# State-space heads: score products run two heads at a time, decays on ScalarE, and GpSimd low parts with later transposes in the expert search

## The chip, the cores and the metric

One core of one Trainium2 chip runs the whole kernel. The metric is device time in microseconds (us) of one execution; lower is better. TensorE has two clock levels here, 1.2 and 2.4 GHz; the profile writes the granted clock as a share of 2.4 GHz.

## What is computed

256 tokens (and 16 meta tokens ahead of them) of width 1024 pass through a hybrid layer (a gated linear attention and a state-space mixer, "SSD"), a layer of product-key experts ("PEER"), and a second block of retention and stick-breaking attention. Two parts of it matter here. The SSD's core, for a chunk:

```python
acum = jnp.cumsum(a, axis=1)
seg = jnp.exp(-jnp.abs(acum[:, :, None] - acum[:, None, :]))
cb = jnp.einsum('btgn,bsgn->btsg', Cc, Bc)
y = jnp.einsum('btsgr,btsg,bsgrp->btgrp', seg, cb, xdt)
y = y + jnp.einsum('btgn,bgrpn,btgr->btgrp', Cc, S, jnp.exp(acum))
```

There are 32 heads in 4 groups of 8. And the search of the experts: for each token and head the 16 best of 128 first keys and of 128 second keys, and of their sums the 16 best again:

```python
s = jnp.einsum('nhid,hikd->nhik', q, sub_keys).astype(jnp.float32)
s_top, i_top = lax.top_k(s, PEER_TOPK)
cand = s_top[:, :, 0, :, None] + s_top[:, :, 1, None, :]
best, pos = lax.top_k(cand.reshape(n, PEER_HEADS, PEER_TOPK * PEER_TOPK), PEER_TOPK)
```

after which the activations of all 16384 experts are formed with the whole table `u`, 128 experts at a time, and weighed.

## The kernel before

Weights stream from memory in blocks of 128 x 1024 values (`_stream`, lines 72 to 83): a DMA into `raw`, ScalarE rounds it to `whi` (line 80), and VectorE or GpSimd forms the rest, `wlo = raw - whi` (line 82). Each of the three has three buffers, so the `whi` of a block waits for the end of the block three places ahead. `_proj` (lines 91 to 108) multiplies such a block with activations that are split in the same way: 8 times the three products hi*hi, hi*lo, lo*hi, 24 matmuls. Which engine forms `wlo` is a count (`_low`: every fourth on GpSimd), or in the experts' loop a rule by block number, `k.u_low` (line 1385).

The order of the instructions on each engine is fixed when the program is built: a scheduler puts them in the order of its own estimate of when they become ready, within the dependencies. `tc.issue_after(x)` makes the instructions of a block stand behind instruction x on x's engine. Every engine then works through its list in order, and each instruction waits for what it needs.

The SSD (class `Group`, lines 460 to 574) takes the 4 groups one after the other; each has 4 pairs of heads, i = 0 to 3. For each group: `conv` projects and convolves six tiles (B, C and four of x); `prepare` turns x by TensorE transposes into `xdt`, forms the meta tokens' part and the scores `cbm` = C B; `decays(i)` gets a row of cumulated decays for each of two heads by one matmul into `prow`, subtracts the column's own value and gives it the sign on VectorE (`scalar_tensor_tensor`, line 527, twice a head), takes exponentials on ScalarE (lines 529, 530), and multiplies by `cbm` on GpSimd (line 531) into `M` (128 x 384). `heads(i, Ms)` makes the pair's output with six fp32 matmuls into one tile `py`: two of `xbd` (line 541), two of `M`'s first 256 columns (line 543), two of its last 128 (line 546). Each of these has a stationary operand of 64 columns, and the two heads use different halves of the array. `gate(i)` projects z and multiplies on GpSimd (line 558), `norm` splits the result into `yhi` and `ylo` (lines 572 to 574). The loop at lines 585 to 607 interleaves the convolutions of the next group with the heads of this one.

The experts (`_stage2`): after the queries, the loop at line 876 goes over 128 blocks of `u`, b = 0 to 127, 24 matmuls each. Beside the first 44 of them VectorE runs the search (`_topk`, lines 678 to 760, a generator that is advanced by `choose(b)`), once for each half of the tokens. When a half is done, `turn` (line 749) turns its keys and weights by three transposes on TensorE; `choose` puts them behind a block four blocks after the search's last step (line 836). In this loop `wlo` is formed on GpSimd in four blocks of five below b = 44 (VectorE has b = 0, 5, 10, ...), then in every second one.

Of the kernel before, what the change touches and what calls it, by code (L numbers as in the profile page):

```python
# [11 lines left out]
F32 = mybir.dt.float32  # L12
# [4 lines left out]
OP = mybir.AluOpType  # L17
# [124 lines left out]
def _stage1(k, a):  # L142
# [7 lines left out]
    def c1(name, rows=P):  # L150
        s, n = CONST_COLS[name]
        return cb_[:rows, s - N_CONST_A:s - N_CONST_A + n]
# [160 lines left out]
    nc.tensor.matmul(pa[:, 64:96], c1("gt"), aN[:, 1], start=True, stop=True)  # L313
    nc.tensor.matmul(pa[:, 96:128], c1("repgt", NM), aN[:NM, 0], start=True, stop=True)
    acs = base.tile([P, 3, H32], F32, name="acs")
    nc.vector.tensor_copy(acs, pa[:, :96].rearrange("p (j h) -> p j h", j=3))
    revx = base.tile([P, SG, SR], F32, name="revx")
    nc.vector.tensor_tensor(revx, pa[:, 96:128].rearrange("p (g r) -> p g r", g=SG),
                            c1("rmask")[:, None, :].to_broadcast([P, SG, SR]), op=OP.mult)
# [140 lines left out]
    class Group:  # L460
# [19 lines left out]
            nc.vector.scalar_tensor_tensor(dst, th, 1.0, acc, op0=OP.add, op1=OP.mult)  # L480

        def prepare(self):
            g, BT, CT, xs = self.g, self.BT, self.CT, self.xs
            self.xdt = xdt = sd.tile([P, 2, 512], F32, tag="xdt", bufs=2, name="xdt")
            for j in range(2):
                px = ps.tile([P, 512], F32, tag="sm", name="px")
                for i in range(4):
                    nc.tensor.transpose(px[:, i * P:(i + 1) * P], xs[:, i, NM + j * P:NM + (j + 1) * P], cst("ident"))
                nc.vector.tensor_tensor(xdt[:, j].rearrange("p (r d) -> p r d", r=SR),
                                        px.rearrange("p (r d) -> p r d", r=SR),  # L490
                                        dtN[:, j + 1, g * SR:(g + 1) * SR, None].to_broadcast([P, SR, SP]), op=OP.mult)
            px = ps.tile([P, 512], F32, tag="sm", name="px")
            for i in range(4):
                xrep = sd.tile([P, SR, NM], F32, tag="xrep", bufs=2, name="xrep")
                nc.gpsimd.tensor_copy(xrep, xs[:, i, None, :NM].to_broadcast([P, SR, NM]))
                nc.tensor.transpose(px[:, i * P:(i + 1) * P], xrep.rearrange("p r s -> p (r s)"), cst("ident"))
            self.xbd = sd.tile([P, 512], F32, tag="xbd", bufs=2, name="xbd")
            nc.vector.tensor_tensor(self.xbd.rearrange("p (r d) -> p r d", r=SR), px.rearrange("p (r d) -> p r d", r=SR),
                                    dtm[:, g, :, None].to_broadcast([P, SR, SP]), op=OP.mult)
            brep = sd.tile([P, SR, NM], F32, tag="brep", bufs=1, name="brep")  # L500
            nc.gpsimd.tensor_copy(brep, BT[:, None, :NM].to_broadcast([P, SR, NM]))
            pm2 = ps.tile([P, 512], F32, tag="sm", name="pm2")
            nc.tensor.matmul(pm2[:, :T], sel[:, g * SR:(g + 1) * SR].rearrange("p r s -> p (r s)"), rows[:, 1],
                             start=True, stop=True)
            nc.tensor.matmul(pm2[:, T:], brep.rearrange("p r s -> p (r s)"), CT[:, NM:], start=True, stop=True)
            self.mm = mm = sd.tile([P, T], F32, tag="mmeta", bufs=2, name="mmeta")
            nc.scalar.activation(mm, pm2[:, :256], AF.Exp, bias=revm[:, g:g + 1])
            nc.vector.tensor_mul(mm, mm, pm2[:, 256:512])

            pcb = ps.tile([P, 512], F32, tag="sm", name="pcb")  # L510
            nc.tensor.matmul(pcb[:, 0:256], BT[:, NM:NM + P], CT[:, NM:], start=True, stop=True)
            nc.tensor.matmul(pcb[:, 256:384], BT[:, NM + P:], CT[:, NM + P:], start=True, stop=True)
            self.cbm = cbm = sd.tile([P, 3, P], F32, tag="cbm", bufs=2, name="cbm")
            for j in (0, 2):
                nc.vector.tensor_mul(cbm[:, j], pcb[:, j * P:(j + 1) * P], c1("blk"))
            nc.vector.tensor_copy(cbm[:, 1], pcb[:, P:2 * P])

        def decays(self, i):

            Ms = []  # L520
            for q in range(2):
                h = self.g * SR + 2 * i + q
                prow = ps.tile([P, 512], F32, tag="sm", name="prow")
                nc.tensor.matmul(prow[:, :T], idr[:, h:h + 1].to_broadcast([P, P]), rows[:, 0], start=True, stop=True)
                M = sd.tile([P, 3, P], F32, tag="M", bufs=4, name="M")
                for j in range(2):
                    nc.vector.scalar_tensor_tensor(M[:, 2 * j], prow[:, j * P:(j + 1) * P], acs[:, j, h:h + 1],
                                                   c1("sgn"), op0=OP.subtract, op1=OP.mult)
                nc.scalar.activation(M[:, 1], prow[:, P:2 * P], AF.Exp, bias=acs[:, 2, h:h + 1])
                nc.scalar.activation(M[:, 0::2], M[:, 0::2], AF.Exp)  # L530
                nc.gpsimd.tensor_mul(M, M, self.cbm)
                Ms.append(M)
            return Ms

        def heads(self, i, Ms):
            xdt = self.xdt
            py = ps.tile([P, 512], F32, tag="sm", name="py")
            yo = [py[q * SP:(q + 1) * SP] for q in range(2)]
            cols = [slice((2 * i + q) * SP, (2 * i + q + 1) * SP) for q in range(2)]
            for q in range(2):  # L540
                nc.tensor.matmul(yo[q][:, :T], self.xbd[:, cols[q]], self.mm, start=True, stop=False)
            for q in range(2):
                nc.tensor.matmul(yo[q][:, :T], xdt[:, 0, cols[q]], Ms[q][:, 0:2].rearrange("p a b -> p (a b)"),
                                 start=False, stop=False)
            for q in range(2):
                nc.tensor.matmul(yo[q][:, P:T], xdt[:, 1, cols[q]], Ms[q][:, 2], start=False, stop=True)
            yv = self.xs[:, i, NM:]
            c = 4 * self.g + i
            nc.vector.scalar_tensor_tensor(yv, yv, par("ssd_d")[:, c:c + 1], py[:, :T], op0=OP.mult, op1=OP.add)

        def gate(self, i):

            pz = _proj(k, [a["w_z"][4 * self.g + i]], xh, xl)
            sz = sd.tile([P, T], F32, tag="sz", bufs=2, name="sz")
            nc.scalar.activation(sz, pz[:, :T], AF.Tanh, scale=0.5)
            nc.vector.scalar_tensor_tensor(sz, sz, 1.0, pz[:, :T], op0=OP.add, op1=OP.mult)
            yv = self.xs[:, i, NM:]
            nc.gpsimd.tensor_mul(yv, yv, sz)
            if i == 0:
                self.sqs = sd.tile([P, T], F32, tag="sqs", bufs=2, name="sqs")  # L560
                nc.scalar.activation(self.sqs, yv, AF.Square)
            else:
                s2 = sd.tile([P, T], F32, tag="s2", bufs=1, name="s2")
                nc.scalar.activation(s2, yv, AF.Square)
                nc.gpsimd.tensor_add(self.sqs, self.sqs, s2)
# [24 lines left out]
    for g in range(SG):  # L590
        G1 = Group(g + 1) if g + 1 < SG else None
        for i in range(4):
            if G1 and i < 3:
                G1.conv(2 * i)
                G1.conv(2 * i + 1)
            if i < 3:
                nxt = G0.decays(i + 1)
            elif G1:
                G1.prepare()
                nxt = G1.decays(0)  # L600
            if not G1:
                gates(i)
            G0.heads(i, Ms)
            Ms = nxt
            G0.gate(i)
        G0.norm()
        G0 = G1

# [69 lines left out]
def _topk(k, tp, num16, sc, j, T1, T2, Wh, Wl):  # L678
# [35 lines left out]
        nc.vector.max_index(pos[:, h, 8:16], best[:, h, 8:16], rest)  # L714
        yield 5

    w = tp.tile([P, PH, KT], F32, tag="w", bufs=1, name="w")
    nc.vector.tensor_tensor(w, best, best[:, :, 0:1].to_broadcast([P, PH, KT]), op=OP.subtract)

    ab = tp.tile([P, 2, PH, KT], U32, tag="ab", bufs=1, name="ab")  # L720
# [4 lines left out]
    nc.vector.scalar_tensor_tensor(abf[:, 1], pos, float(ROWS * KT), ab[:, 1], op0=OP.is_lt, op1=OP.mult)  # L725
    act(w, w, AF.Exp)
    yield 5
    key = tp.tile([P, 2, PH, KT], F32, tag="key", bufs=1, name="key")
    full = [P, PH, KT, KT]
    for i in range(2):  # L730
        pair = tp.tile([P, 2, PH, KT, KT], F16, tag="big", bufs=2, name="pick")
# [40 lines left out]
def _stage2(k, a):  # L772
# [52 lines left out]
    def choose(b):  # L825
        nonlocal left
        for at, turn in [x for x in turns if x[0] <= b]:
            turn()
        turns[:] = [x for x in turns if x[0] > b]
        left += PER_BLOCK  # L830
        while left > 0:
            step = next(steps, None)
            if step is None:
                return not turns
            if isinstance(step, tuple):
                turns.append((b + 4, step[1]))
                step = step[0]
            left -= step
        return False
# [537 lines left out]
def tile_block(ctx, tc, out, a):  # L1377
# [3 lines left out]
    k.turn = 0  # L1381
    k.ahead = 0
    k.pool_every = 4
    k.P_FIRST, k.P_LAST = 44, 122
    k.u_low = lambda b: "gpsimd" if (b % 5 if b < k.P_FIRST else b % 2) else "vector"
    cp = ctx.enter_context(tc.tile_pool(name="consts", bufs=1))
    k.mhalf = cp.tile([P, 16], F32, name="mhalf")
    nc.vector.memset(k.mhalf, -0.5)
# [171 lines left out]
```

## Time and profile before

| | |
|---|---|
| median of 3 runs | 1673.63 us (1672.87 to 1674.48) |
| profiled execution | 1673.89 us, its span 1672.1 us |
| TensorE busy | 1644.6 us, 98% of the span |
| VectorE, ScalarE, GpSimd busy | 1175.5, 843.4, 477.0 us |
| mean of a block's `whi` on ScalarE, `wlo` on VectorE, `wlo` on GpSimd | 1.06, 1.25, 2.55 us |
| HBM | 164 GB/s over the span, DMA engines half busy |
| granted TensorE clock | 0.996 of full speed |

The profile's parts are: busy time by engine, the span in 40 slices, DMA queues, the chain of work that ended last, and groups of equal instructions with the idle time of their engine ahead of them. A wait is put down to the instruction that released it. The SSD's heads lie between about 155 and 345 us, the first 44 blocks of `u` between 493 and 629 us. "PEld" is the loading of stationary operands.

### The profile page before, as it was taken

The numbers are of one execution on the slowest core, as the hardware profiler recorded it, in microseconds if no ns is written. First come the engines' busy times: TensorE is split into PE (matmuls) and PEld (weight loads), VectorE is DVE, ScalarE is ACT, GpSimd is POOL, SyncE is SP. The second block draws the span as 40 slices with busy tenths as digits, with TensorE's granted clock in tenths as the row PEclk, the third lists the DMA queues.
The fourth block names the chain that finished last, engine by engine and source line by source line (L and its number), as shares of the span: only waits on it lengthen the run. The fifth ranks groups of instructions, "written<-read, shape, count | busy, mean of one in ns | idle before, by whom it ended". The sixth has DMA issues, their size and how long they took to land.

```text
span 1672.1 us, 28941 instructions
## 1 busy us (share of the span) xinstructions
PE 1644.6 (98%) x11268; PEld 1499.5 (90%) x11268; DVE 1175.5 (70%) x2018; ACT 843.4 (50%) x1394; POOL 477.0 (29%) x320
## 2 busy tenths in 40 slices
PE   7999999999999999999999999999999999999998
PEld 5899998999999999999999888888888888798996
DVE  7668797546879759899997555555557775667454
ACT  4545555444545464544445545545445444566543
POOL 4223555421236664343342000000007331011110
PEclk9999999999999999999999999999999999999999
DMA  5333433455545455455445565655656445554543
GB/s 182 112 127 124 129 126 126 144 175 189 192 159 168 157 186 165 160 165 160 161 152 189 193 196 190 195 194 192 196 180 202 161 160 176 175 164 136 169 161 127
DMA packets 76680, 276.45 MB, mean 165 GB/s; under 512 B 8512, under 2 KB 9664, under 8 KB 76288
## 3 DMA queue, kind: packets, MB, share of 16 engines
q1 hardware_dynamic: 75392, 271.36, 50.1%
q10 hardware_dynamic: 1152, 3.26, 0.6%
q8 instruction: 88, 1.44, 0.4%
q14 instruction: 48, 0.39, 0.1%
HBM read 273.54 MB, written 1.05 MB: 164 GB/s over the span
## 4 chain that ended last, share of the span: by engine, by line
PE 89%; DVE 7%; DMA 1%; issue 1%; ACT 1%; POOL 1%; POOLq 0%; DVEq 0%; ACTq 0%
PE mm L104 15%; PE mm L106 14%; PE mm L105 14%; PE acc L918 7%; PE acc L917 7%; PE acc L916 7%; PE rows L128 2%; PE rows L127 2%; PE rows L130 2%; PE ytok L1000 1%; PE ytok L1001 1%; PE pp L863 1%; PE pg L104 1%; PE pg L106 1%; PE pg L105 1%
## 5 line engine op out<-in xcount | busy, mean ns | idle before, releaser
L80 ACT ACTIVATE whi<-raw 128x1024 fp32r<-128x1024 f32 x506 | 535.6, 1059 | 618.0 <-PE mm L105 269.4
L82 DVE TENSOR_TENSOR wlo<-raw,whi 128x1024 fp32r<-128x1024 f32 x380 | 475.6, 1252 | 308.9 <-ACT whi L80 304.7
L82 POOL TENSOR_TENSOR wlo<-raw,whi 128x1024 fp32r<-128x1024 f32 x126 | 320.5, 2546 | 557.1 <-ACT whi L80 493.7
L104 PE MATMUL mm<-bh,whi 128*128 128x256 f32 x1024 | 293.8, 287 | 0.0
L106 PE MATMUL mm<-bh,wlo 128*128 128x256 f32 x1024 | 290.8, 284 | 2.7 <-DVE wlo L82 2.5
L105 PE MATMUL mm<-bl,whi 128*128 128x256 f32 x1024 | 290.6, 284 | 0.0
L106 PEld LDWEIGHTS mm<-bh,wlo 128*128 128x128 f32 x1024 | 197.3, 193 | 3.2 <-DVE wlo L82 2.8
L917 PE MATMUL acc<-wlo,wv 128*128 128x512 f32 x512 | 199.2, 389 | 0.0
L918 PE MATMUL acc<-whi,wv 128*128 128x512 f32 x512 | 199.2, 389 | 0.0
L104 PEld LDWEIGHTS mm<-bh,whi 128*128 128x128 f32 x1024 | 197.6, 193 | 0.1
L105 PEld LDWEIGHTS mm<-bl,whi 128*128 128x128 f32 x1024 | 197.6, 193 | 0.0
L104 PE MATMUL mm<-hh,whi 128*128 128x256 f32 (+1 forms) x576 | 166.4, 289 | 0.9 <-DVE acc L475 0.9
L106 PE MATMUL mm<-hh,wlo 128*128 128x256 f32 (+1 forms) x576 | 166.2, 289 | 0.0
L105 PE MATMUL mm<-hl,whi 128*128 128x256 f32 (+1 forms) x576 | 164.9, 286 | 0.0
L916 PE MATMUL acc<-whi,wv 128*128 128x512 f32 x512 | 137.3, 389 | 0.0
L918 PEld LDWEIGHTS acc<-whi,wv 128*128 128x128 f32 x512 | 96.1, 188 | 20.0
L916 PEld LDWEIGHTS acc<-whi,wv 128*128 128x128 f32 x512 | 96.1, 188 | 19.9
L917 PEld LDWEIGHTS acc<-wlo,wv 128*128 128x128 f32 x512 | 96.1, 188 | 19.9
L104 PEld LDWEIGHTS mm<-hh,whi 128*128 128x128 f32 x576 | 108.4, 188 | 6.0 <-issue 3.1
L964 POOL TENSOR_TENSOR sq<-sq,s 128x256 f32<-128x256 f32 x6 | 8.1, 1360 | 361.2 <-ACT s L962 361.2
L106 PEld LDWEIGHTS mm<-hh,wlo 128*128 128x128 f32 x576 | 108.6, 189 | 2.4 <-issue 2.2
L105 PEld LDWEIGHTS mm<-hl,whi 128*128 128x128 f32 x576 | 108.5, 188 | 0.9 <-issue 0.8
(539 smaller groups left out, 3493.7 us busy)
## 6 DMA issues: line engine op xcount, KB each, us to landing
raw<-in_u_dram SPq DMA_DIRECT2D x128, 512.0 KB, 3.6
raw<-in_v_dram SPq DMA_DIRECT2D x128, 512.0 KB, 4.3
raw<-in_w_xbc_dram SPq DMA_DIRECT2D x24, 512.0 KB, 3.5
raw<-in_w_z_dram SPq DMA_DIRECT2D x16, 512.0 KB, 3.5
raw<-in_w_up_ssd_dram SPq DMA_DIRECT2D x16, 512.0 KB, 4.2
raw<-in_w_q_dram SPq DMA_DIRECT2D x16, 512.0 KB, 3.7
raw<-in_ret_v_dram SPq DMA_DIRECT2D x16, 512.0 KB, 3.2
raw<-in_ret_qk_dram SPq DMA_DIRECT2D x16, 512.0 KB, 3.7
```

The lines of the kernel that those rows point to most:

```text
L80: k.last_whi = nc.scalar.activation(hi[:, :cols], raw[:, :cols], AF.Copy).ins
L82: k.last_wlo = eng.tensor_sub(lo[:, :cols], raw[:, :cols], hi[:, :cols]).ins
L104: nc.tensor.matmul(out[:m, :n], wh, xh[:, j], start=(j == 0), stop=False)
L105: nc.tensor.matmul(out[:m, :n], wh, xl[:, j], start=False, stop=False)
L106: last = nc.tensor.matmul(out[:m, :n], wl, xh[:, j], start=False, stop=(j == nb * 8 - 1))
L127: nc.tensor.matmul(out[:e - s], xh[:, j, s:e], wh, start=(j == 0), stop=False)
L128: nc.tensor.matmul(out[:e - s], xh[:, j, s:e], wl, start=False, stop=False)
L130: nc.tensor.matmul(out[:e - s], xl[:, j, s:e], wh, start=False, stop=(j == nb * 2 - 1))
L863: nc.tensor.matmul(pp[:, i * P:(i + 1) * P], o1[:, q, :, r], wh[:, q, :, r], start=True, stop=False)
L916: nc.tensor.matmul(o, wh[:, t], hi[:, v], start=(b == 0), stop=False)
L917: nc.tensor.matmul(o, wh[:, t], lo[:, v], start=False, stop=False)
L918: nc.tensor.matmul(o, wl[:, t], hi[:, v], start=False, stop=(b == NE - 1))
```

## The change

- `acs` is stored with its sign turned, so that `decays` gets the absolute difference by ScalarE's `Abs` with a bias in place of VectorE's subtract and multiply; the exponential then has scale -1. The multiplication by `cbm` goes from GpSimd to VectorE.
- `heads` and `prepare` stand under `tc.issue_after(k.last_mm)`, and `heads` sets `k.last_mm` to its own last matmul, so that they aren't spread between the matmuls of a projection that was written ahead of them. In the loop `decays(i + 1)` comes ahead of the convolutions, and for i = 3 the gate's projection ahead of the heads and `prepare` behind them. `xrep` has three buffers.
- In the experts' loop GpSimd forms `wlo` in all blocks below b = 38 and VectorE in 38 to 43; the transposes of a half come no earlier than b = 38, and `w` and `key` have two buffers.

```diff
-    nc.vector.tensor_copy(acs, pa[:, :96].rearrange("p (j h) -> p j h", j=3))
+    nc.vector.tensor_scalar_mul(acs[:, :2], pa[:, :64].rearrange("p (j h) -> p j h", j=2), -1.0)
+    nc.vector.tensor_copy(acs[:, 2], pa[:, 64:96])
...
         def prepare(self):
+            with tc.issue_after(k.last_mm):
+                self._prepare()
+
+        def _prepare(self):
...
-                xrep = sd.tile([P, SR, NM], F32, tag="xrep", bufs=2, name="xrep")
+                xrep = sd.tile([P, SR, NM], F32, tag="xrep", bufs=3, name="xrep")
...
                 for j in range(2):
-                    nc.vector.scalar_tensor_tensor(M[:, 2 * j], prow[:, j * P:(j + 1) * P], acs[:, j, h:h + 1],
-                                                   c1("sgn"), op0=OP.subtract, op1=OP.mult)
+                    nc.scalar.activation(M[:, 2 * j], prow[:, j * P:(j + 1) * P], AF.Abs, bias=acs[:, j, h:h + 1])
                 nc.scalar.activation(M[:, 1], prow[:, P:2 * P], AF.Exp, bias=acs[:, 2, h:h + 1])
-                nc.scalar.activation(M[:, 0::2], M[:, 0::2], AF.Exp)
-                nc.gpsimd.tensor_mul(M, M, self.cbm)
+                nc.scalar.activation(M[:, 0::2], M[:, 0::2], AF.Exp, scale=-1.0)
+                nc.vector.tensor_mul(M, M, self.cbm)
...
         def heads(self, i, Ms):
+            with tc.issue_after(k.last_mm):
+                self._heads(i, Ms)
+
+        def _heads(self, i, Ms):
...
-                nc.tensor.matmul(yo[q][:, P:T], xdt[:, 1, cols[q]], Ms[q][:, 2], start=False, stop=True)
+                k.last_mm = nc.tensor.matmul(yo[q][:, P:T], xdt[:, 1, cols[q]], Ms[q][:, 2], start=False, stop=True).ins
...
         for i in range(4):
+            if i < 3:
+                nxt = G0.decays(i + 1)
             if G1 and i < 3:
                 G1.conv(2 * i)
                 G1.conv(2 * i + 1)
-            if i < 3:
-                nxt = G0.decays(i + 1)
-            elif G1:
+            if not G1:
+                gates(i)
+            early = G0.gate(i) if i == 3 else None
+            G0.heads(i, Ms)
+            if G1 and i == 3:
                 G1.prepare()
                 nxt = G1.decays(0)
-            if not G1:
-                gates(i)
-            G0.heads(i, Ms)
             Ms = nxt
-            G0.gate(i)
+            G0.gated(i, early or G0.gate(i))
...
-    w = tp.tile([P, PH, KT], F32, tag="w", bufs=1, name="w")
+    w = tp.tile([P, PH, KT], F32, tag="w", bufs=2, name="w")
...
-    key = tp.tile([P, 2, PH, KT], F32, tag="key", bufs=1, name="key")
+    key = tp.tile([P, 2, PH, KT], F32, tag="key", bufs=2, name="key")
...
-                turns.append((b + 4, step[1]))
+                turns.append((max(b + 4, k.P_FREE), step[1]))
...
-    k.P_FIRST, k.P_LAST = 44, 122
-    k.u_low = lambda b: "gpsimd" if (b % 5 if b < k.P_FIRST else b % 2) else "vector"
+    k.P_FREE, k.P_FIRST, k.P_LAST = 38, 44, 122
+    k.u_low = lambda b: "gpsimd" if b < k.P_FREE or (b >= k.P_FIRST and b % 2) else "vector"
```

`gated` is the second half of what was `gate`. The order of the built programs shows what the scheduler makes of it. First TensorE in the first group of the SSD, where the second pair's products stand; `mm` is a projection's output, `py` the pair's. Before:

```order
L541 MATMUL py<-mmeta,xbd 64x256 x2
L104 MATMUL mm<-hh,whi 128x256
L105 MATMUL mm<-hl,whi 128x256
L106 MATMUL mm<-hh,wlo 128x256
L104 MATMUL mm<-hh,whi 128x256
L105 MATMUL mm<-hl,whi 128x256
L543 MATMUL py<-M,xdt 64x256
L106 MATMUL mm<-hh,wlo 128x256
L104 MATMUL mm<-hh,whi 128x256
L105 MATMUL mm<-hl,whi 128x256
```

The rest of the pair follows seven projection matmuls later. With the change, the last pair of the first group and the next group's `prepare` behind it (`px` are the transposes, `pm` the meta tokens' part; line numbers are the changed kernel's):

```order
L105 MATMUL mm<-hl,whi 128x256
L106 MATMUL mm<-hh,wlo 128x256
L552 MATMUL py<-mmeta,xbd 64x256 x2
L554 MATMUL py<-M,xdt 64x256 x2
L557 MATMUL py<-M,xdt 64x128 x2
L495 MATMUL px<-csta,xs 128x128 x6
L503 MATMUL px<-csta,xrep 128x128 x3
L510 MATMUL pm_2190<-rows,sel 128x256
L512 MATMUL pm_2190<-CT,brep 128x256
```

The six products stand together, and the transposes have moved from places of their own to behind them. Over the 16 pairs the products stood in 28 pieces before and stand in 20 now; 12 pairs are whole.

Then VectorE beside the experts' blocks, in the search of the second half of the tokens, before:

```order
L692 MAX v_6653<-rest 128x8 x2
L693 MAX_INDEX i_6654<-v_6653,rest 128x8 x2
L691 MATCH_REPLACE rest<-v_6653,sc_5217 128x128 x2
L692 MAX v_6653<-rest 128x8
L82 TENSOR_TENSOR wlo<-raw,whi 128x1024
L692 MAX v_6653<-rest 128x8
L693 MAX_INDEX i_6654<-v_6653,rest 128x8 x2
```

and with the change, at the search's end:

```order
L758 TENSOR_TENSOR key<-pick 128x128
L82 TENSOR_TENSOR wlo<-raw,whi 128x1024 x2
L754 TENSOR_TENSOR pick<-pick 128x2048
L82 TENSOR_TENSOR wlo<-raw,whi 128x1024
L757 TENSOR_TENSOR pick<-pick 128x8x128
L771 CAST keys<-ptk 128x128
L772 CAST keys<-ptk 128x128
L773 TENSOR_SCALAR wgts<-ptk 128x128
```

The `wlo` among the search's steps before is that of b = 15. With the change none of b = 0 to 37 is in VectorE's list; the first two there, near the search's end, are those of b = 38 and 39. On TensorE the first half's transposes (`ptk`) stood behind 23 blocks of `u` and stand behind 39; the second half's stand behind 43 in both.

## Rows read from the trace of the kernel before

**Rows 1.** Page, busy time by engine: us, share of the span, instructions.
```profile
PE 1644.6 (98%) x11268; PEld 1499.5 (90%) x11268; DVE 1175.5 (70%) x2018; ACT 843.4 (50%) x1394; POOL 477.0 (29%) x320
```

**Rows 2.** Page, the chain that ended last, by engine.
```profile
PE 89%; DVE 7%; DMA 1%; issue 1%; ACT 1%; POOL 1%; POOLq 0%; DVEq 0%; ACTq 0%
```

**Rows 3.** Windows of the SSD's heads and the search: length, busy us (instructions) of PE, PEld, DVE, ACT, POOL; clock; DMA.
```profile
155.00:345.00 190.00, 188.19 (x1482) 171.17 (x1480) 140.45 (x271) 103.88 (x207) 101.75 (x93) 1.00 0.42 133
490.00:626.00 136.00, 131.16 (x1067) 130.49 (x1067) 101.12 (x355) 72.95 (x101) 91.37 (x35) 0.97 0.53 169
```

**Rows 4.** Waits of PE, 155 to 345 us: total us, times, longest.
```profile
PE mm L104 <- DVE acc L475: 0.9, 1, 0.9
PE py L541 <- ACT M L529: 0.6, 1, 0.6
PE py L543 <- POOL M L531: 0.4, 1, 0.4
```

**Rows 5.** Timeline of PE, a pair in one piece: start us, us, instruction.
```profile
196.17 0.29 PE L105 MATMUL mm<-hl,whi 128*128 128x272 f32 x1
196.39 0.65 PE L541 MATMUL py<-mmeta,xbd 128*64 128x256 f32 x4
...
197.62 0.39 PE L106 MATMUL mm<-hh,wlo 128*128 128x272 f32 x1
197.85 0.29 PE L104 MATMUL mm<-hh,whi 128*128 128x272 f32 x1
```

**Rows 6.** Timeline of PE, first piece of a pair in three pieces.
```profile
170.64 0.28 PE L106 MATMUL mm<-hh,wlo 128*128 128x272 f32 x1
170.85 0.65 PE L541 MATMUL py<-mmeta,xbd 128*64 128x256 f32 x4
171.44 0.39 PE L104 MATMUL mm<-hh,whi 128*128 128x256 f32 x1
171.66 0.28 PE L105 MATMUL mm<-hl,whi 128*128 128x256 f32 x1
```

**Rows 7.** Groups by line and shape, 155 to 345 us: busy us, mean ns; idle before.
```profile
L529 ACT ACTIVATE M<-prow,acs 128x128 f32<-128x128 f32 x32 | 11.6, 363 | 9.9 <-DVE M L527 9.4 <-PE mm L104 0.5
L527 DVE SCALAR_TENSOR_TENSOR M<-prow,acs,cstb 128x128 f32<-128x128 f32 x64 | 18.7, 341 | 1.4 <-POOL M L531 1.0 <-PE prow L524 0.5
L574 DVE TENSOR_TENSOR ylo<-xs,yhi 128x256 fp32r<-128x256 f32 x12 | 10.1, 864 | 0.0
L489 DVE TENSOR_TENSOR xdt<-px,dtN 128x512 f32<-128x512 f32 x8 | 5.1, 685 | 3.2 <-PE px L488 3.2
L508 DVE TENSOR_TENSOR mmeta<-mmeta,pm 128x256 f32<-128x256 f32 x4 | 1.6, 410 | 0.0
L531 POOL TENSOR_TENSOR M<-M,cbm 128x384 f32<-128x384 f32 x32 | 40.5, 1280 | 22.6 <-ACT M L530 20.0 <-DVE M L527 1.7 <-DVE acc L475 0.8
```

**Rows 8.** Timelines of POOL and of DVE about 258 us.
```profile
257.69 2.40 POOL L82 TENSOR_TENSOR wlo<-raw,whi 128x1024 fp32r<-128x1024 f32 x1 [6.48 <-ACT whi L80]
258.04 2.33 DVE L574 TENSOR_TENSOR ylo<-xs,yhi 128x256 fp32r<-128x256 f32 x1
```

**Rows 9.** Waits of PE, 490 to 640 us.
```profile
PE mm L106 <- DVE wlo L82: 2.5, 1, 2.5
PE ptk L752 <- DVE key L742: 2.4, 1, 2.4
```

**Rows 10.** Windows of PE, projections' tile mm alone: length, busy us (matmuls), clock, DMA.
```profile
536.61:571.22 34.61, 29.32 (x218) 0.90 0.46 153
571.22:605.78 34.56, 34.56 (x290) 1.00 0.56 175
623.07:629.16 6.09, 6.01 (x50) 1.00 0.72 237
```

**Rows 11.** Groups by line, POOL, 490 to 626 us.
```profile
L82 POOL TENSOR_TENSOR wlo<-raw,whi 128x1024 fp32r<-128x1024 f32 x35 | 91.4, 2619 | 49.9 <-ACT whi L80 49.6
```

**Rows 12.** Timeline of POOL, its longest wlo among these.
```profile
544.77 4.52 POOL L82 TENSOR_TENSOR wlo<-raw,whi 128x1024 fp32r<-128x1024 f32 x1 [3.10 <-ACT whi L80]
```

More of the change, by code (lines that the diff above doesn't have):

```diff
@@ L556, in gate, with gated @@
             nc.vector.scalar_tensor_tensor(sz, sz, 1.0, pz[:, :T], op0=OP.add, op1=OP.mult)
+            return sz
+        def gated(self, i, sz):
             yv = self.xs[:, i, NM:]
```

## Prediction

> **What bounds the kernel.** I read the busy times first, then the chain, then windows of the two places that the change touches, then TensorE's waits in them, and last its timeline. TensorE is busy for 98% of the span [rows 1] and has 89% of the chain that ended last [rows 2], so time is won only where TensorE waits, runs slowly, or does something that it needn't; work that leaves another engine is worth nothing by itself. In the heads' window (155 to 345 us) TensorE is busy for 188.2 of 190 us and VectorE, the next, for 140.5; in the search's window (490 to 626) TensorE is busy for 131.2 of 136 [rows 3]. So the heads offer little waiting, the search some 5 us of it. The clock says more: in the search it is granted at 0.97 on the mean, in the heads at 1.00 [rows 3].
>
> **Search: what is removed.** A block of `u` is 24 matmuls. From 571.22 to 605.78 us twelve blocks (288 matmuls and two at the edges) take 34.56 us, 2.88 a block; from 536.61 to 571.22 the nine before them take 34.61 [rows 10]. Nine blocks at 2.88 are 25.92, so 8.69 us are lost there. Two waits begin it: 2.5 us for a `wlo` of VectorE, 2.4 for the keys that the first half's transposes turn [rows 9]. The rest, 3.8, is mostly the clock, 0.90 on the mean over the stretch and 1.00 behind it [rows 10]: after each of the waits it falls to its lower level for a while. Both waits have one cause: VectorE works through a fixed list in which these `wlo` and keys stand behind search steps that take longer than the scheduler thought.
>
> The change takes both away. The `wlo` of b = 15, 20 and 25 go to GpSimd, and the transposes go from behind block 23 to behind block 39, some 45 us later, while VectorE's list loses six `wlo`. The transposes still have to be made: the second half's, behind block 43, lie in two blocks that take 6.09 us in place of 5.76 [rows 10], so 0.33 us. Gain: 8.69 - 0.33 = 8.4 us.
>
> **Search: what is added.** GpSimd has 38 blocks in a row. It takes 2.62 us for one [rows 11] against the 2.88 of a block, and waits for ScalarE between them, 49.9 us over the window [rows 11], so it keeps up with 0.26 us a block to spare. But its longest took 4.52 us [rows 12], beside VectorE's steps. A block's `whi` can be formed as soon as the block three places ahead ends, so `wlo` has two blocks, 5.76 us, less ScalarE's 1.06 (the table of the time before): one of 4.52 us is just in time, two in a row are late by some 1.6 us, and if that lets the clock fall the price is that of a wait now. Bounds: 0 and about 4.3 us (half of 8.69, one of the two waits come back). I take 0.5, since the mean is nearer to the good end. VectorE's blocks 38 to 43 stand behind the search's last steps; VectorE has 101 of 136 us in this window [rows 3], and six blocks of 1.25 us (the same table) replace as many that it had earlier. Nothing for these. Search: **-7.9 us**.
>
> The Trainium skill speaks against this part (SBUF — State Buffer, section "Who interferes with whom"): a VectorE instruction with two SBUF inputs and a GpSimd instruction that reads SBUF exclude each other, the later one being fully blocked. The trace agrees: beside a 2.40 us `wlo` on GpSimd a VectorE subtraction of 128 x 256 took 2.33, where that size takes 0.41 on line 508 [rows 7], and it ended 0.28 us behind GpSimd's [rows 8]. What it would make of the whole change is the third rival below.
>
> **Heads: what is removed.** The price of a piece of products follows from two timelines. A pair in one piece: from the projection matmul ahead of it to the second behind it 197.85 - 196.17 = 1.68 us, where two matmuls apart by 0.12 would stand 0.24 apart; so 1.44 us [rows 5]. The first two products alone: 171.66 - 170.64 - 0.24 = 0.78 [rows 6]. Let a piece cost f for going in and out, and a step of 256 columns a (the two heads of a pair run beside each other, so that a pair's product costs as much as one head's), a step of 128 columns a/2. Then f + 2.5a = 1.44 and f + a = 0.78, so a = 0.44 and f = 0.34. Splitting between the heads costs a as well.
>
> Counted in the order of the instructions: before, 28 pieces, 41 long steps (nine pairs are cut between heads) and 17 short ones, and two pieces in which a `prow` matmul stands in the middle, which costs f again: 30 x 0.34 + 41 x 0.44 + 17 x 0.22 = 32.0 us. After, 20 pieces, 35 long steps, 16 short, one such `prow`: 21 x 0.34 + 35 x 0.44 + 16 x 0.22 = 26.1. Gain 5.9 us, all on TensorE and in an order that is fixed. The transposes that move behind the products are single passes either way: nothing.
>
> TensorE's waits here are 1.9 us before [rows 4]; they come from VectorE's row of `M` steps and one `ylo` that was held up [rows 8]. After, the pieces wait for VectorE's multiplication. Bounds: all 1.9 gone, or 5 us of new waits (the 5.9 nearly given back). I take as many as before.
>
> **Heads: what moves between engines.** 64 `Abs` of 128 columns from PSUM on ScalarE: an `Exp` of the same shape takes 0.363 us [rows 7], so 23.2 us on 103.9 of 190 [rows 3]: 127, covered by TensorE's projections. ScalarE also forms `whi`; a pair's four steps of two heads hold it for some 3 us, within the two blocks that a `whi` has. It loses the 9.4 us in which it waited for VectorE's part of `M` [rows 7]. VectorE loses 64 x 0.341 = 21.8 us [rows 7] and gets 32 products of 128 x 384; of its nearest rows 256 columns take 0.41 and 512 take 0.685 [rows 7], so 0.55, 17.6 us in all: 4 less, before waits. GpSimd loses 40.5 of 101.8 us [rows 3, 7]. None of these is on the chain; the cover is TensorE's 188 us, and if it fails the first to be late is a pair's `M`. The sign of `acs` costs one small VectorE instruction once, a DMA nowhere. Heads: **-5.9 us**.
>
> **Sum.** -7.9 - 5.9 = -13.8 us against the profiled execution's 1673.9, so 1660.1; the median of the runs is 0.26 us below that execution. Forecast **1660 us**. At the good ends (8.4 and 7.8) it is 1657.4, and I go to 1656 for GpSimd's relief in the heads, whose price I can't see. At the bad ends (4.1 and 0.9 or so) it is 1668 to 1669.
>
> **Rivals.**
> First: the heads' gain goes into waits. A piece in one run can't start before the last of its `M` is there, and TensorE's list is in order. For it: the 1.0 us of waits for `M` now [rows 4]. Against it: `decays` stands a whole pair, some 72 matmuls or 8.6 us, ahead. Time: the search's gain alone, 1673.9 - 7.9 = 1666. Chance 0.09.
> Second: GpSimd is late in the search. For it: 4.52 us [rows 12]. Against it: the mean of 2.62 [rows 11]. One wait with its clock comes back: 1660 + 4 = 1664. Chance 0.08. Both together, 1670 or more, is within 0.2% (3.3 us) of no change: 0.04.
> Third, slower: VectorE's multiplications are each held up by GpSimd, and VectorE becomes the bound of the heads. With a full `wlo` of 2.40 us [rows 8] ahead of each, 32 x (0.55 + 2.40) = 94 us on 140.5 - 21.8 = 118.7 are 213 of 190 us: 23 us longer, and 1673.9 - 13.8 + 23 = 1683. VectorE fills 190 - 5.9 = 184 us from (184 - 118.7) / 32 = 2.0 us a product. For it: the 2.33 us case [rows 8]. Against it: `ylo`, which meets GpSimd's work today, takes 0.86 us on the mean [rows 7], 0.45 over those 0.41, and GpSimd will be busy for a third of the window in place of half. Chance 0.04.
>
> **How the numbers follow.** The forecast has 0.75, the rivals 0.09, 0.08, 0.04 and 0.04. About 0.2%, 3.3 us, is what a measurement of this kernel can tell from no change. Faster by more: 0.75 + 0.09 + 0.08 = 0.92; within: 0.04; slower: 0.04. The range runs from 1656 to 1667, with the first two rivals in it; below and above it lies no more than 2 in 10.
>
> **What would show it.** In the search: no wait of TensorE for `wlo` or `key`, granted clock 1.00, 2.88 us a block from b = 2 to 38 and 0.33 us for transposes behind block 39; GpSimd's `wlo` at 2.6 to 2.8 us on the mean. In the heads: whole pairs at 1.44 us, TensorE's waits at 2 us or below, `Abs` near 0.36 us, VectorE's product at 0.55 to 1.0, VectorE busy for less than before. I am wrong if TensorE waits for `wlo` of GpSimd in blocks 10 to 38, if the clock falls again there, or if `py` waits for `M` in many pairs.

## The result, and the profile after

The changed kernel takes **1656.99 us** (median of 4 runs, 1656.13 to 1658.96), the kernel before on the same chip 1674.06 (median of 4, 1672.87 to 1676.36). The ratio is 0.9894, with a 95% interval from 0.988 to 0.9909.

The page's busy times of the changed kernel, and the chain that ended last by engine, answer to [rows 1, 2]:

```profile
PE 1632.8 (99%) x11268; PEld 1493.1 (90%) x11268; DVE 1171.7 (71%) x1984; ACT 856.5 (52%) x1458; POOL 446.2 (27%) x291
```
```profile
PE 92%; DMA 2%; DVE 2%; ACT 1%; issue 1%; POOL 0%; SPq 0%; POOLq 0%; DVEq 0%; ACTq 0%
```

TensorE does as many instructions as before in 11.8 us less of busy time, and its idle time over the span falls by 4.9 us, from 27.5 to 22.6. VectorE's share of the chain falls from 7% to 2%. That share is not time won: 5% of the span is some 84 us, and the span became 16.7 us shorter.

To see where the time went I cut each span at instructions that all kernels have: the first `px` transpose of the SSD, the first matmul of the up-projection, the first block of `u`, and the 47th. The pieces are "ahead", "heads", "between" (always 123.48 us, left out), "search" and "rest". Starts and ends are read from the two traces' timelines of TensorE, in us:

| kernel | ahead | heads | search | rest | span |
|---|---|---|---|---|---|
| before | 153.75 | 215.74 | 141.94 | 1037.18 | 1672.10 |
| after | 151.38 | 207.81 | 134.23 | 1038.49 | 1655.39 |
| difference | -2.4 | -7.9 | -7.7 | +1.3 | -16.7 |

Windows over the stretches of heads and search (length; busy us and instructions of PE, PEld, DVE, ACT, POOL; clock; DMA). Before:

```profile
153.75:369.50 215.75, 213.94 (x1698) 196.86 (x1697) 155.33 (x288) 116.08 (x227) 106.98 (x95) 1.00 0.43 139
492.98:634.92 141.94, 137.10 (x1116) 136.43 (x1115) 108.26 (x358) 76.53 (x106) 93.45 (x36) 0.98 0.52 168
```

After:

```profile
151.38:359.19 207.81, 207.81 (x1698) 195.28 (x1696) 146.13 (x256) 129.16 (x291) 69.88 (x62) 1.00 0.45 144
482.67:616.90 134.23, 134.02 (x1116) 133.67 (x1115) 112.86 (x356) 76.29 (x106) 97.53 (x38) 1.00 0.55 177
```

In the heads TensorE's busy time falls by 213.94 - 207.81 = 6.1 us and its idle time from 1.8 us to nothing. In the search its idle time falls from 4.8 to 0.2 us, and its busy time by 3.1 at the same 1116 matmuls, because the granted clock goes from 0.98 to 1.00.

The waits of TensorE agree. There is none between 150 and 345 us, where [rows 4] had three. Between 475 and 640, where [rows 9] had two of some 2.5 us, one is left:

```profile
PE mm L106 <- POOL wlo L82: 0.2, 1, 0.2
```

### The profile page after: what moved, and what is told of

Read it like the earlier page. It is cut to its first block, busy times and chain, and to the rows that moved or that the text cites. A ratio compares the mean times of both kernels' runs of the same rounds, so it can differ in the third digit from the quotient of the medians.

```text
span 1655.4 us, 28879 instructions
## 1 busy us (share of the span) xinstructions
PE 1632.8 (99%) x11268; PEld 1493.1 (90%) x11268; DVE 1171.7 (71%) x1984; ACT 856.5 (52%) x1458; POOL 446.2 (27%) x291
## 3 DMA queue, kind: packets, MB, share of 16 engines
q8 instruction: 88, 1.44, 0.3%
HBM read 273.54 MB, written 1.05 MB: 166 GB/s over the span
## 4 chain that ended last, share of the span: by engine, by line
PE 92%; DMA 2%; DVE 2%; ACT 1%; issue 1%; POOL 0%; SPq 0%; POOLq 0%; DVEq 0%; ACTq 0%
PE mm L104 16%; PE mm L106 16%; PE mm L105 16%; PE acc L933 7%; PE acc L932 7%; PE acc L934 7%; PE rows L128 2%; PE rows L127 2%; PE rows L130 2%; PE ytok L1016 1%; PE ytok L1017 1%; PE pp L879 1%; PE pg L104 1%; PE pg L106 1%; PE pg L105 1%
## 5 line engine op out<-in xcount | busy, mean ns | idle before, releaser
L82 DVE TENSOR_TENSOR wlo<-raw,whi 128x1024 fp32r<-128x1024 f32 x377 | 468.4, 1243 | 287.8 <-ACT whi L80 285.7
L82 POOL TENSOR_TENSOR wlo<-raw,whi 128x1024 fp32r<-128x1024 f32 x129 | 326.6, 2536 | 562.5 <-ACT whi L80 492.4
```

Source lines behind the costliest of these rows:

```text
L82: k.last_wlo = eng.tensor_sub(lo[:, :cols], raw[:, :cols], hi[:, :cols]).ins
```

## The experiments

E1 to E11 are the changed kernel or the kernel before, with one thing altered. Runs with one time are read by their stretches and not by that time: the times of the kernel before, on the chips used, ran from 1671.3 to 1678.2, more than most of the effects.

### E1 and E2: one half of the change at a time

E1 is the changed kernel with the old search; E2 is the kernel before with the new one. E2 against before (E1 makes the opposite edit in after):

```diff
...
-    k.u_low = lambda b: "gpsimd" if (b % 5 if b < k.P_FIRST else b % 2) else "vector"
+    k.u_low = lambda b: "gpsimd" if b < k.P_FREE or (b >= k.P_FIRST and b % 2) else "vector"
...
-                turns.append((b + 4, step[1]))
+                turns.append((max(b + 4, k.P_FREE), step[1]))
```

(and `w` and `key` with two buffers). Expected of E1:

> The heads' part of the change alone; the experts' search as before. Theory: the two parts don't touch, so the stretch from the first px transpose to the first up-projection matmul takes 207.8 us as in the whole change (215.8 before), the search loses its 8.7 us as before, and the time is 1674.1 - 7.9 = 1666.1 us. Rival: the 2.4 us that were won ahead of the heads and the 1.6 that were lost behind the search belong to the change too; then the first px stands 2.4 us earlier here as well.

Expected of E2:

> The search's part alone; the heads as before. Theory: from the first block of u to block 46 it takes 134.2 us (141.9 before), no wait of TensorE for wlo or key, clock 1.00 there, and the time is 1674.1 - 7.7 = 1666.4 us. Rival: the search gained because it began 10 us earlier against the table's DMAs; then it stays near 141.9.

| kernel | ahead | heads | search | rest | median of 4 | ratio to before, 95% |
|---|---|---|---|---|---|---|
| E1 | 151.40 | 207.82 | 142.21 | 1037.04 | 1664.52 | 0.9941 (0.9919 to 0.9963) |
| E2 | 151.91 | 215.76 | 134.46 | 1036.23 | 1663.55 | 0.9937 (0.9915 to 0.996) |

Each half changes its own stretch and leaves the other as it was. The whole times fall by more, 11.3 and 12.3 us against the kernel before on that chip, but with intervals of some 6 to 14 us that take in the 7.9 and the 7.5 of the stretches. The 2.4 us ahead of the heads belong to neither half: E1 has them, as the rival would, but E2, whose code there is that of before, starts its heads at 151.91 too. Over all thirteen kernels that point lies between 151.2 and 153.8 and "rest" between 1036.1 and 1039.1, with no code changed in either, so the 2.4 and the 1.3 are scatter.

### E3 and E4: one edit of the search at a time

E3 has only the new rule for `wlo`, E4 only the late transposes with their buffers.

> Only the rule by which GpSimd forms wlo below block 38; the transposes as before behind block 23. Theory: both waits have one cause, VectorE's late list. Without the wait at block 15 the transposes are reached 4.4 us earlier while the keys come only some 2.4 to 3.7 us earlier (two or three wlo fewer ahead of them), so the wait for key stays at 2.5 to 4.5 us and the gain is 2 to 4.5 us. Rival: the two edits add up, the wait for key goes with the wlo of VectorE, and this edit alone gives 7 to 8 us.

> Only the transposes behind block 39 in place of 23 (with the two buffers of w and key); wlo as before. Theory: the wait for wlo at block 15 stays at 2.5 us with its clock; the wait for key goes, but then block 25, whose wlo stands behind the search in VectorE's list, comes 4 us earlier and waits up to 3 us itself, so the gain is 0 to 2 us. Rival: the edits add up and this one gives its 3.9 us.

Neither brings any of the gain: the search takes 144.55 us in E3 and 146.04 in E4, against 141.94 before. Together, in E2, they give 134.46. That each alone makes the search slower isn't shown: with both edits left out it took 142.21 us in E1 and 145.21 in E9 (below), and E3 and E4 are one execution each. TensorE's waits between 488 and 640 us, of E3:

```profile
PE ptk L752 <- DVE key L742: 7.7, 2, 5.5
PE mm L106 <- POOL wlo L82: 0.2, 1, 0.2
```

and of E4:

```profile
PE mm L106 <- DVE wlo L82: 8.5, 2, 6.1
```

The traces say why. Times from the first block of `u` (b counts from 0):

| | before | E3 | E4 | after |
|---|---|---|---|---|
| VectorE ends the first half's first key | 68.0 | 72.9 | 68.0 | 72.9 |
| VectorE ends its second key | 73.7 | 75.7 | 73.9 | 83.2 |
| VectorE ends the `wlo` of b = 25 | 80.5 | none | 83.3 | none |
| TensorE starts b = 20 | 62.1 | 58.8 | 62.1 | 58.7 |
| TensorE starts b = 25 | 81.1 | 83.7 | 76.9 | 73.1 |

In E4 the keys are no longer waited for, so TensorE comes to b = 25 4.2 us sooner, and that block's `wlo` ends 2.8 us later: 83.3 - 76.9 = 6.4 us, of which TensorE waits 6.1. In E3 TensorE is 3.3 us sooner at b = 20. It waits 5.5 us for the first key, which comes 4.9 us **later** than before, and 2.3 for the second, the one that was waited for before, which comes 2.1 us later. Yet VectorE has five `wlo` fewer ahead of them (b = 0, 5, 10, 15 and 20, 6.1 us). Search steps that read two tiles of SBUF take longer beside a GpSimd that forms `wlo` all the time, while the `MAX8` steps (one tile) keep their 0.27 us. The group of one such step, up to 566 us, before:

```profile
L738 DVE TENSOR_TENSOR pick<-pick 128x2048 f16<-128x2048 f16 x2 | 2.4, 1204 | 0.0
```

and in E3:

```profile
L738 DVE TENSOR_TENSOR pick<-pick 128x2048 f16<-128x2048 f16 x2 | 5.4, 2680 | 0.0
L747 DVE TENSOR_TENSOR w<-w,smx 128x128 f32<-128x128 f32 x1 | 1.5, 1475 | 0.0
```

(`w` took 0.28 us before.) This is what the Trainium skill says (SBUF — State Buffer, "Who interferes with whom"): a VectorE instruction with two SBUF inputs and a GpSimd instruction that reads SBUF shut each other out. The traces agree. In the changed kernel the first key comes as late as in E3, at 72.9, and the second at 83.2, but neither is needed before b = 39 starts, at 113.7. So the late transposes are not a second saving beside the GpSimd edit but its cover.

My expectations failed in their gains: I had E3 as worth 2 to 4.5 us and E4 as 0 to 2, and neither gained. The waits that I named, for the key in E3 and for b = 25 in E4, came, but longer (7.7 and 6.1 us, where I had up to 4.5 and 3). A wait also costs more than itself. E3's window that begins in its wait of 5.5 us (columns as above):

```profile
561.00:571.20 10.20, 4.84 (x22) 4.58 (x23) 10.17 (x41) 0.09 (x1) 2.78 (x1) 0.50 0.34 108
```

The clock is at the lower of its two levels for 10.2 us; before, each wait of 2.4 or 2.5 us had 3.4 us of it. The row also shows why the second key follows so soon here: while TensorE waits, blocks don't end, ScalarE forms next to no `whi`, GpSimd is busy for only 2.8 us, and VectorE's steps are short again. Its `pick` of 128 x 1024 for the second key takes 0.68 us in E3 and 2.90 in after, where nothing waits.

### E5: no fixed order behind the products

```diff
-            with tc.issue_after(k.last_mm):
-                self._heads(i, Ms)
+            self._heads(i, Ms)
```

(the same in `prepare`).

> The whole change without the two issue_after: the scheduler may again spread a pair's products between a projection's matmuls. Counted in its order: 23 pieces, 39 long steps, 16 short, one prow in the middle, 28.8 us by the prices of the prediction against 26.1. Theory: the heads' stretch (first px transpose to first up-projection matmul; 215.7 us before, 207.8 with the change) is 207.8 + 2.7 = 210.5 us, with no wait of TensorE in it. Rival: pieces cost nothing by themselves and the gain came from the moved engines; then 208.

Heads: 210.62 us, 2.8 more than after, with no wait of TensorE. The scheduler cuts the products into pieces again, and the count at f = 0.34 and a = 0.44 gave 210.5. (E5's trace has two `prow` matmuls in the middle, not the one that I counted; with both it is 210.9.) The rival's 208 is refuted.

### E6, E9 and E8: which engine matters

E6 is the changed kernel with differences on VectorE and products on GpSimd as before; E9 the kernel before with only the new engines; E8 the changed kernel with the products alone put back (the sign of `acs` and of the exponential goes with the differences):

```diff
 # E6 against after; E9 makes the opposite edit in before
-                    nc.scalar.activation(M[:, 2 * j], prow[:, j * P:(j + 1) * P], AF.Abs, bias=acs[:, j, h:h + 1])
+                    nc.vector.scalar_tensor_tensor(M[:, 2 * j], prow[:, j * P:(j + 1) * P], acs[:, j, h:h + 1],
+                                                   c1("sgn"), op0=OP.subtract, op1=OP.mult)
...
 # E6 and E8 against after
-                nc.vector.tensor_mul(M, M, self.cbm)
+                nc.gpsimd.tensor_mul(M, M, self.cbm)
```

> The whole change, but the differences of decays on VectorE and the products with the scores on GpSimd, as before. Counted: 22 pieces, 35 long, 16 short, one prow in the middle, 26.7 us. Theory: the moved engines bring only the waits (1.9 us before), so the heads' stretch is 207.8 + 0.6 to 2.5 = 208.4 to 210.3 us. Rival: without them VectorE and GpSimd hold the pairs that now stand in one run, with waits of 3 us or more for M, and the stretch is over 211.

> The kernel before with the moved engines alone (Abs on ScalarE, product on VectorE), neither issue_after nor the loop's new order, nor the search's part. Counted: 26 pieces, 40 long, 16 short, one prow in the middle, 30.3 us against 32.0. Theory: the heads' stretch is 215.7 - 1.7 by pieces, less up to 1.9 of waits: 212.1 to 214.0 us. Rival: the engines are the larger part of the gain, 210 or less.

> The whole change with the product of the scores left on GpSimd; the differences are on ScalarE. Counted: 22 pieces, 38 long steps, 16 short, none in the middle, 27.7 us. Theory: VectorE is freed either way, the heads' stretch is 207.8 + 1.6 = 209.4 us, plus at most 1 us of waits for GpSimd. Rival: GpSimd's product of 1.2 us beside its wlo makes the pairs late, 2 us or more of waits for M.

| kernel | heads | against before | TensorE's waits in them |
|---|---|---|---|
| E9, engines alone | 212.57 | -3.2 | none |
| E6, order alone | 218.32 | +2.6 | 5.8 us |
| E8, order and `Abs`, products on GpSimd | 208.93 | -6.8 | none |
| after | 207.81 | -7.9 | none |

E6's waits of TensorE, 150 to 372 us:

```profile
PE mm L104 <- DVE acc L477: 5.8, 2, 3.3
```

and windows of E6 about the ends of these two waits (columns as above):

```profile
216.00:220.40 4.40, 3.70 (x18) 3.70 (x19) 4.40 (x12) 1.71 (x5) 0.52 (x2) 0.61 0.52 142
260.70:267.50 6.80, 5.33 (x23) 5.33 (x24) 4.48 (x11) 1.92 (x6) 5.54 (x6) 0.50 0.47 151
```

With the order alone the pieces are fewer, but VectorE, which still has its 64 differences, is late with the convolution's `acc`, for which the next projection waits; the clock falls behind it. Of the first window's matmuls 3.04 us stand at half the clock, of the second's all 5.33: they lose about 4.2 us. With the waits (5.8) and the 0.6 counted for its pieces that is 10.6, and E6's distance from after is 10.5. The stretch is on the rival's side of the expectation, over 211, but the waits are for `acc` and none is for `M`: the engines are needed, for another reason than it gave. E8 says that one of the two engine edits is enough: with the differences on ScalarE and the products still on GpSimd no wait is left, and the 1.1 us that it loses against after are by the count its pieces (1.6). Its time in all, 1656.30 us, lies within the runs of after. Whether the products' move alone would do was not run. By the groups, GpSimd takes 1288 ns for a product in E8 where VectorE takes 654 in after.

E9's heads lie in the range that was expected and not at its rival's 210 or less. Its search is 145.21 us, 3.3 more than before, with code that is not touched there: TensorE waits 8.5 us for two of VectorE's `wlo`, 7.0 of it for one, that of b = 20, which ends 67.4 us after the first block, before 62.8. VectorE's list has the same instructions in the same order as before there. What differs is which engine comes first where VectorE and GpSimd meet. The first step whose time differs much is `abf`. Timeline of VectorE and GpSimd, before:

```profile
523.55 2.49 DVE L725 SCALAR_TENSOR_TENSOR abf<-pos,ab 128x128 f16<-128x128 uint32 x1
523.47 2.41 POOL L82 TENSOR_TENSOR wlo<-raw,whi 128x1024 fp32r<-128x1024 f32 x1 [0.47 <-ACT whi L80]
```

and in E9:

```profile
518.60 0.28 DVE L725 SCALAR_TENSOR_TENSOR abf<-pos,ab 128x128 f16<-128x128 uint32 x1
518.80 3.49 POOL L82 TENSOR_TENSOR wlo<-raw,whi 128x1024 fp32r<-128x1024 f32 x1 [0.75 <-ACT whi L80]
```

From there on the two meet at other places. Of the steps ahead of b = 20's `wlo`, `cand` (128 x 1024) takes 3.27 us in E9 and 1.20 before, and `pick` (128 x 2048) 3.43 and 1.21. So the old search can come out 3 us apart with the same lists; in the eight kernels with the whole new one it took 134.1 to 134.8 us.

### E7: one head after the other

```diff
             for q in range(2):
                 nc.tensor.matmul(yo[q][:, :T], self.xbd[:, cols[q]], self.mm, start=True, stop=False)
-            for q in range(2):
                 nc.tensor.matmul(yo[q][:, :T], xdt[:, 0, cols[q]], Ms[q][:, 0:2].rearrange("p a b -> p (a b)"),
...
-            for q in range(2):
                 k.last_mm = nc.tensor.matmul(yo[q][:, P:T], xdt[:, 1, cols[q]], Ms[q][:, 2], start=False, stop=True).ins
```

> The whole change with a pair's six products written head by head, so that two steps which follow each other on TensorE no longer use different halves of the array, except where one head's last meets the next one's first. Counted: 22 pieces, 64 long steps, 32 short: 43.0 us against 26.1. Theory: a pair's step costs as much as one head's, so the heads' stretch is 207.8 + 16.9 = 224.7 us. Rival: the halves don't run beside each other and only the number of pieces counts: 208.5 us.

Heads: 215.43, 7.6 more than after, between the two theories. Timeline of TensorE over one pair (start, length, instruction) of after:

```profile
306.76 0.28 PE L106 MATMUL mm<-hh,wlo 128*128 128x256 f32 x1
306.97 0.65 PE L552 MATMUL py<-mmeta,xbd 128*64 128x256 f32 x4
307.45 0.60 PE L554 MATMUL py<-M,xdt 128*64 128x256 f32 x4
307.89 0.39 PE L557 MATMUL py<-M,xdt 128*64 128x128 f32 x4
308.20 0.38 PE L104 MATMUL mm<-hh,whi 128*128 128x256 f32 x1
308.43 0.28 PE L105 MATMUL mm<-hl,whi 128*128 128x256 f32 x1
```

and of E7:

```profile
313.52 0.28 PE L106 MATMUL mm<-hh,wlo 128*128 128x256 f32 x1
313.74 0.65 PE L552 MATMUL py<-mmeta,xbd 128*64 128x256 f32 x2
314.22 0.38 PE L553 MATMUL py<-M,xdt 128*64 128x256 f32 x1
314.22 0.43 PE L552 MATMUL py<-mmeta,xbd 128*64 128x256 f32 x1
...
315.14 0.38 PE L555 MATMUL py<-M,xdt 128*64 128x128 f32 x2
315.45 0.39 PE L104 MATMUL mm<-hh,whi 128*128 128x256 f32 x1
315.67 0.28 PE L105 MATMUL mm<-hl,whi 128*128 128x256 f32 x1
```

In after a pair takes 308.43 - 306.76 - 0.24 = 1.43 us, the 1.44 of [rows 5]. In E7 it takes 315.67 - 313.52 - 0.24 = 1.91, where the six products one by one would have made it 0.34 + 5 x 0.44 = 2.5. The reason stands in the two rows at 314.22: the first head's second step and the second head's first step start together, on the two halves of the array. So heads do run beside each other, and steps need not be the same ones; what costs here is a step that finds no partner.

### E10: GpSimd busier in the heads

```diff
+    k.pool_every = 2
     for g in range(SG):
...
+    k.pool_every = 4
     for c in range(4, KD):
```

GpSimd forms every second `wlo` there in place of every fourth.

> The whole change, but in the loop over the groups GpSimd forms wlo in every second block in place of every fourth, so that VectorE's products of scores meet it twice as often. Counted: 23 pieces, 36 long steps, 16 short, no prow in the middle, 27.2 us against 26.1. Theory: VectorE's product of 128 x 384 goes from 0.65 us on the mean to about 0.9, hidden behind TensorE's projections; the heads' stretch is 208.5 to 209.5 us and TensorE waits there for less than 1 us. Third rival of the prediction: the products are held up by whole wlo of 2.4 us, take over 1.5 us on the mean, and TensorE waits 5 us or more: 214 or more.

Heads: 208.86 us, 1.05 more than after, with no wait of TensorE: the scheduler's list has the products in more pieces (23, after has 20), for which the count had 1.1. VectorE's product takes longer, if less than the 0.9 us that I expected, by this group of E10 (150 to 345 us):

```profile
L537 DVE TENSOR_TENSOR M<-M,cbm 128x384 f32<-128x384 f32 x32 | 22.0, 696 | 8.1 <-ACT M L536 8.1
```

against this one of after:

```profile
L537 DVE TENSOR_TENSOR M<-M,cbm 128x384 f32<-128x384 f32 x32 | 20.4, 654 | 4.4 <-ACT M L536 4.4
```

Even so it is far from the 2.0 us at which VectorE would fill the stretch. The third rival is refuted here.

### E11: every pair whole

```diff
...
-        for kk in range(8):
+        with k.tc.issue_after(k.last_mm) if k.pin else ExitStack():
+            for kk in range(8):
...
```

with `k.pin` true in the heads from the second pair on, so that no projection slips into a pair.

> The whole change, and from the second pair of the first group on a projection's matmuls too stand behind the last matmul of the projection or pair written ahead of them, so that 15 of 16 pairs stand whole. Counted: 17 pieces, 34 long steps, 16 short, prow in the middle of four, 25.6 us against 26.1. Theory: the heads' stretch is 207.3 us, and the time that of the whole change within its noise. Rival: pairs that can't be cut wait for M, 1 to 3 us, and the stretch is 208 to 211.

15 of 16 pairs are whole, where the trace of after has 13 (one more than the section on the change says), but the heads take 207.92 us, as in after (207.81), with a wait of 0.3. The median is 1657.2 (1656.95 to 1657.64, 4 runs), the ratio to before 0.9886 (0.987 to 0.9903): no better than the change. The 0.5 us by which I had it shorter didn't show.

## Why the prediction was right, and where it was not

**Pieces: right.** Forecast 5.9 us, and TensorE's busy time in the heads fell by 6.1. The price of a piece held to some 0.6 us: 210.5 counted and 210.62 measured in E5, 208.9 and 208.86 in E10, 209.4 (and up to 1 more) and 208.93 in E8, 207.3 and 207.92 in E11, where 0.3 is a wait. In E9 I counted 212.1 to 214.0 and measured 212.57, but its trace has two more cuts than I counted, by transposes; with them it is 212.8 to 214.7. It was too simple in one place: a for a step of one head alone holds at the edge of a piece, not inside a run (E7).

**TensorE's waits in the heads: the step that failed.** "I take as many as before", 1.9 us; none are left, and the heads gained 7.9, the good end of 7.8. E9 shows that the engines' part takes them away, in the old order too; E8 shows that of it the differences' move to ScalarE is enough. I had bounded this on both sides and chosen a middle, though the cause that I named for them, VectorE's row of `M` steps, is what the change removes. This is 2.0 of the 2.9 us by which the profiled execution came out below the forecast. The rest is luck: scatter in stretches that the change doesn't touch (-2.4 and +1.3), less the 0.2 that the search fell short. What the two edits do alone I had not asked: order without engines makes the heads slower (E6).

**Search: right in size.** 7.7 us against 7.9. The keys are not waited for. The transposes cost what I had, 0.33 us at each of their two places: b = 42 and 43 take 3.13 and 2.95 in place of 2.88 each, and b = 37 to 39 take 8.97 in place of 8.64. GpSimd's lateness was priced at 0.5 and is 0.68: b = 18 and 19 take 3.09 and 3.35 us. After's timeline of TensorE at b = 19:

```profile
538.63 0.39 PE L106 MATMUL mm<-bh,wlo 128*128 128x256 f32 x1 [0.21 <-POOL wlo L82]
```

and of GpSimd about it, up to 545 us, five in a row that take 2.87 us each:

```profile
532.82 14.34 POOL L82 TENSOR_TENSOR wlo<-raw,whi 128x1024 fp32r<-128x1024 f32 x5 [2.04 <-ACT whi L80]
```

Its mean is as expected, by the group of 480 to 616 us:

```profile
L82 POOL TENSOR_TENSOR wlo<-raw,whi 128x1024 fp32r<-128x1024 f32 x39 | 101.6, 2621 | 37.8 <-ACT whi L80 37.6
```

It waits for ScalarE 37.8 us in all, so it kept up, and the second rival, with its lost clock, didn't happen. My margin for it had a slip: two of 4.52 us in a row would be late by 2 x 4.52 - (4.70 + 2.88) = 1.5 us, not 1.6.

**What I got wrong about why.** I wrote that VectorE's list loses six `wlo` and gets as many at its end, as if the keys came sooner for it. It loses eight (b = 0 to 35) and gets five, and the keys still come later: the first by 4.9 us (E3, after), the second by 2.1 in E3 and 9.5 in after. Only the late transposes make that harmless. The mechanism of my third rival, GpSimd in VectorE's way, is real; it strikes in the search, where 30 to 40 us of slack take it (keys at 72.9 and 83.2, needed at 113.7).

**Durations.** `Abs` took 384 ns (I took 363), the product 654 (I took 550), by these groups of after; `ylo`, no longer held up so often, 553 where [rows 7] have 864:

```profile
L534 ACT ACTIVATE M<-prow,acs 128x128 f32<-128x128 f32 x64 | 20.4, 384 | 6.6 <-PE prow L531 4.5 <-PE py L557 2.2
L589 DVE TENSOR_TENSOR ylo<-xs,yhi 128x256 fp32r<-128x256 f32 x13 | 6.9, 553 | 0.1
```

None of the three is on the path: TensorE has no idle time in the stretch.

## What to carry to other kernels

Where an in-order list on one engine feeds another, taking away the first late item brings the consumer sooner to the next one; price the edits of such a list together, each against the new arrival times, since one alone can bring nothing of what both save (E3, E4). When work goes to GpSimd, look at what VectorE does at that moment, not only at whether GpSimd keeps up: here the steps that stayed on VectorE and read two tiles of SBUF grew. Where the two engines meet often, one trace doesn't give the worth of an edit: unchanged lists gave searches of 141.94, 142.21 and 145.21 us. And where an edit removes the very instructions that a wait stands behind, take the wait as gone unless a row names who is late next.

## What the runs showed of the hardware that I had not expected

- A wait costs more than its length, by an amount that doesn't follow its length. About each wait TensorE's clock stood at its lower level for a while, part of it within the wait. The time in which matmuls ran at that level, halved, estimates what the clock added:

| wait, us | clock at the lower level, us | matmuls in it, us | added, us (estimate) |
|---|---|---|---|
| before, 2.5 | 3.4 | 3.05 | 1.5 |
| before, 2.4 | 3.4 | 3.16 | 1.6 |
| E6, 2.5 | 3.4 | 3.04 | 1.5 |
| E6, 3.3 | 6.8 | 5.36 | 2.7 |
| E4, 6.1 | 6.8 | 3.83 | 1.9 |
| E9, 7.0 | 10.2 | 6.01 | 3.0 |
| E3, 5.5 and 2.3 | 10.2 | 4.84 | 2.4 |

  The windows of E4 and of E9:

```profile
573.01:579.84 6.83, 3.83 (x18) 3.83 (x19) 2.95 (x3) 0.00 (x0) 0.53 (x1) 0.50 0.42 130
551.24:561.48 10.24, 6.01 (x28) 6.01 (x29) 10.24 (x50) 1.13 (x2) 0.48 (x1) 0.50 0.45 154
```

  The shorter waits here, after's 0.2 us, the 0.4 to 0.9 of [rows 4] and one of 1.5 in E9, had none.
- The stretch ahead of the heads, which no edit touches, can lose clock too. Before, 40 to 60 us:

```profile
40.00:60.00 20.00, 20.00 (x90) 13.14 (x88) 14.68 (x23) 17.02 (x20) 3.54 (x2) 0.91 0.35 107
```

  and after:

```profile
40.00:60.00 20.00, 19.68 (x103) 13.10 (x102) 14.36 (x26) 17.63 (x21) 3.93 (x4) 1.00 0.39 122
```

  Of the thirteen kernels only before and E4 show the dip, and they are the two that reach the heads latest (153.75 and 153.41 us). Why it comes in some executions was not tried.
- Two products that each use half of the array's columns run beside each other even where they are different steps of a pair (E7, both at 314.22 us).
- Where VectorE and GpSimd both read SBUF, some tenths of a microsecond decide which of them waits: GpSimd's `wlo` came 0.08 us ahead of `abf` before, which then took 2.49 us, and 0.20 us behind it in E9, where `abf` took 0.28 and the `wlo` 3.49 in place of 2.41.
